# A hybrid decoder layer on one core: the sums of w_out's quarters, the norms' roots and the load of A12 placed anew

## The chip, the core and the metric

The kernel runs on one core of a Trainium2 chip, in float32. The metric is the device time of one execution in microseconds (us), the median of several executions. A program here issues instructions to TensorE (PE, matmuls; PEld is its weight load), VectorE (DVE), ScalarE (ACT), GpSimd (POOL) and SyncE (SP), which issues nearly all transfers (DMAs). Each engine works through its own queue in order.

## The reference, cut to what matters

```python
h = rms_norm(x, norm_gain) * (1.0 + scale) + shift          # shift, scale, gate from silu(c) @ W_ada + b_ada
proj = h @ w_in                                             # 1024x2048 @ 2048x8192
q_sb, k_sb, v_sb, z_sb, q_r, k_r, v_r, z_r = split(proj)    # 1024 columns each, 8 heads of 128
oa = stick_breaking_attention(rms_norm(q_sb), rms_norm(k_sb), v_sb) * silu(z_sb)
ob = head_group_norm(chunkwise_retention(rotary(q_r), rotary(k_r) * HD ** -0.5, v_r)) * silu(z_r)
y = concatenate([oa, ob]) @ w_out                           # 1024x2048 @ 2048x2048
return x + gate * y
```

## The kernel before, in words

**Products.** Every large product is float32 in three matmuls of 128x512 (`mm3`, L185 to L188): both factors are cut into a high and a low part (ScalarE copies the high part, VectorE subtracts it, L173 to L182), and high x high, high x low and low x high are added in PSUM. Both large products use a scheme of seven products of quarters in the place of eight: sums of quarters of the left and the right factor are multiplied. For the output, the right factor's quarters are B11, B12, B21 and B22 of w_out, and its sums T1 = B12 - B11, T2 = B22 - T1 = B22 - B12 + B11, T3 = B22 - B12 and T4 = B21 - T2. The left factor's quarters A11, A12, A21 and A22 are those of the concatenated heads, its sums S1 to S4.

**Order of the work.** TensorE's order is written out by hand. First come the norm and one seventh of the projection, then seven groups of columns (56 or more entries of 12 matmuls each, `run_entry`), then the output. Beside the groups' products run tasks that the clock of half steps (`tick`, twice an entry) pushes on: `later(n, fn)` enters `fn` n half steps later, ahead of the tasks of that half step and in the order in which it was asked for; a generator that yields n goes on n half steps later. The engines' queues hold instructions in the order in which they are entered so. The tasks are:

- `prepare(h)` (L970) and `sb_attention(h)` for the attention heads, two in each of groups 1 to 4. A score matmul of a head comes every three half steps; `scored` holds the half step of the last one, and whoever needs its PSUM bank A0 waits for `scored + 2`. `prepare` makes the norms of q and k: squares, sums over the partitions by matmul (`nm`), transposes (`ntp`), and in `roots` (L1011) an inverse square root by a first guess and three Newton steps of three small VectorE operations each (`rsqrt_newton`, L160). Four half steps after the transposes `y` is transposed itself (L1022).
- `sb_attention`: scores; one half step later sigmoids on ScalarE, three later `products` (L1112) on VectorE; `turn` (L1129) transposes the weights into banks B and A1, whose high and low parts are cut one and two half steps later (`lows`, L1161, with L1164).
- `gate_steps` (L883): the row of gates, from group 1 on. `bias_steps` (L851), from group 2 on: the bias of one column block in two halves, each with 16 loads, sums on VectorE (L864), one matmul per head (`zs`, L872) and copies (L874 to L878). At its end follow `sum_steps` (L938): for each of 8 row blocks k and 2 column blocks m, it loads B22, B12 and B11 of w_out (L946), makes T3, T1 and T2 (L950) and stores each to DRAM (L952).
- `ret_heads`: the eight retention heads, after the attention heads, from group 5 on (`ret_attention`, L1271, 21 half steps a head). Loads come six half steps before their rotation on VectorE (L1250 to L1255); `chain` (L1311, L1317) makes the states that `values` (L1336, L1343) multiplies; `stats` copies the result (L1348) and sums it, `roots` (L1360) and `norm` finish it, and a store to `concat` (L1383) frees its slot.
- `pump` (L262) loads the factors of the coming entries (L273, L275, and L260 through `load_raw`) whenever slots are free.

**Slots.** 92 slots of 128x512 are dealt in classes ("att" 30, "raw" 24, "ring" 24, "dst" 14) and given out first in, first out. A slot is put back when its last use is entered, so a new tile waits for the old one's last reader, a store too. An empty class "att" or "dst" borrows from the fullest.

**The output** has 64 steps (L1445): product 7 (T3) in two column halves of 8 steps, 12 matmuls a step; then products 1 (B11), 6 (T2), 5 (T1), 3 (B22), 2 (B21) and 4 (T4) of 8 steps, 24 matmuls a step. At step i the loads of the right factor for step i + 6 are issued (`load_right`, L1471), sums for step i + 4 made (`sum_right`, L1483; before only T4 = B21 - T2), and cuts for step i + 3 (`cut_right`, `cut_left`). `plan` (L1546) sets at which step the quarters A are loaded, multiplied with silu(z) (`times_z`) and summed (`left_sum`). Finished banks are copied or added (`evac_o`, L1643), with the last operations in `fin`.

Of the kernel before, what the change touches and what calls it, by code (L numbers as in the profile page):

```python
# [11 lines left out]
F32 = mybir.dt.float32  # L12
# [5 lines left out]
P = 128  # L18
S = 1024
# [32 lines left out]
class Slots:  # L52
# [25 lines left out]
    def get(self, name, cls=None, dtype=F32, borrow=False):  # L78
        q = self.free.get(cls) or self.free[None]
        if not q and (borrow or self.loose or cls in ("att", "dst")):  # L80
            q = max(self.free.values(), key=len)
        assert q, (name, cls, {c: len(f) for c, f in self.free.items()})
        i = q.popleft()
        t = self.pool.tile([P, HALF], dtype, tag=f"s{i}", name=name)
        self.of[id(t)] = (t, i)
        return t

    def put(self, *tiles):
        for t in tiles:
# [9 lines left out]
def layer_kernel(ctx, tc, x, c, w_ada, b_ada, norm_gain, w_in, sb_q_gain, sb_k_gain, ret_norm_gain, w_out,  # L99
# [18 lines left out]
    proj = {f"{n}{h}": dr.tile([P, S], F32, name=f"pr_{n}{h}") for n in ("q", "k", "z", "v", "rk", "rv")  # L118
            for h in range(NH)}
    krow = [dr.tile([1, S], F32, name=f"krow{h}") for h in range(NH)]  # L120
    sums_o = {(n, k): dr.tile([P, S], F32, name=f"sum_{n}_{k}") for n in ("T1", "T2", "T3") for k in range(8)}
    fac = {(n, k): dr.tile([P, 2, HALF], F32, name=f"fac_{n}_{k}") for n in RIGHT.values() for k in range(8)}

    def halves(hf):
        return slice(hf * HALF, (hf + 1) * HALF)
# [34 lines left out]
    def rsqrt_newton(y, m, u, iters=3):  # L160

        nc.vector.tensor_scalar(y.bitcast(I32), m.bitcast(I32), -0.5, RSQRT_MAGIC, op0=ALU.mult, op1=ALU.add)
        for _ in range(iters):
            nc.vector.tensor_tensor(u, y, y, op=ALU.mult)
            nc.vector.scalar_tensor_tensor(u, u, -0.5, m, op0=ALU.mult, op1=ALU.mult)
            nc.vector.scalar_tensor_tensor(y, u, 1.5, y, op0=ALU.add, op1=ALU.mult)

    w_in_k = w_in[0].rearrange("(k p) n -> p k n", p=P)

# [8 lines left out]
    def split_to(src, name, cls=None):  # L178

        hi, lo = get(f"{name}h", cls, F32R), get(f"{name}l", cls, F32R)  # L180
        nc.scalar.activation(hi, src, AF.Copy)
        nc.vector.tensor_tensor(lo, src, hi.bitcast(F32), op=ALU.subtract)  # L182
        return hi, lo
# [15 lines left out]
    def later(n, fn):  # L199
        due.setdefault(clock[0] + n, []).append(fn)  # L200
# [650 lines left out]
    def bias_steps():  # L851

        for i in range(2):
            n = min(HALF, NZ * P - i * HALF)
            acc = get(f"qb_acc{i}", "att", borrow=True)
            for kc in range(KC):
                raw = get(f"wb_{kc}_{i}", "att", borrow=True)
                nc.sync.dma_start(raw[:, 0:n], w_in[0][kc * P:(kc + 1) * P, rqcol + i * HALF:rqcol + i * HALF + n])
                yield 4
                a, r, by = acc[:, 0:n], raw[:, 0:n], shift[:, kc:kc + 1]  # L860
                if kc == 0:
                    nc.vector.tensor_scalar(a, r, by, None, op0=ALU.mult)
                else:
                    nc.vector.scalar_tensor_tensor(a, r, by, a, op0=ALU.mult, op1=ALU.add)  # L864
                put(raw)
                yield 1
            while clock[0] < scored[0] + 2:
                yield 1
            hs = slice(4 * i, min(NZ, 4 * i + 4))
            zs = ps.tile([P, NZ], F32, tag="A0", name=f"zs_{i}")  # L870
            for h in range(hs.start, hs.stop):
                nc.tensor.matmul(zs[:, h:h + 1], acc[:, h % 4 * P:(h % 4 + 1) * P], ones[:, 0:1],  # L872
                                 start=True, stop=True)
            nc.vector.tensor_copy(qb[:, 0, hs], zs[:, hs])  # L874
            put(acc)
            yield 2
            nc.scalar.activation(qb[0:64, 1, hs], qb[64:128, 0, hs], AF.Copy)
            nc.scalar.activation(qb[64:128, 1, hs], qb[0:64, 0, hs], AF.Copy)  # L878
        yield 2
        yield from sum_steps()  # L880
# [57 lines left out]
    def sum_steps():  # L938

        for k in range(8):  # L940
            for m in range(2):
                B = {}
                for n in ("B22", "B12", "B11"):
                    f, c_ = k + 8 * (n[1] == "2"), m + 2 * (n[2] == "2")
                    B[n] = get(f"s{n}_{k}_{m}", "att", borrow=True)
                    nc.sync.dma_start(B[n], w_out[0][f * P:(f + 1) * P, halves(c_)])  # L946
                yield 6
                for n, o, a, b, op in (("T3", "B22", "B22", "B12", ALU.subtract),
                                       ("T1", "B12", "B12", "B11", ALU.subtract), ("T2", "B11", "B22", "B11", ALU.add)):
                    nc.vector.tensor_tensor(B[o], B[a], B[b], op=op)  # L950
                    yield 2
                    nc.sync.dma_start(sums_o[n, k][:, halves(m)], B[o])  # L952
                    yield 2
                put(*B.values())

    def run_apart(gen):

# [12 lines left out]
    def prepare(h):  # L970
# [40 lines left out]
        def roots():  # L1011
            u = sm.tile([P, 16], F32, tag="u16", name=f"u16_{h}")
            nc.vector.tensor_scalar(m, m, EPS, None, op0=ALU.add)
            rsqrt_newton(y[:, 0:16], m, u)
            nc.vector.tensor_scalar(y[:, 16:24], y[:, 0:8], -1.0, None, op0=ALU.mult)

        later(1, roots)
        yield 4
        while clock[0] < scored[0] + 2:
            yield 1  # L1020
# [250 lines left out]
    def ret_attention(h, r, gap):  # L1271
# [87 lines left out]

        def roots():  # L1360
            m = sm.tile([P, 8], F32, tag="m8", name=f"m8_{h}")
            nc.vector.tensor_scalar(m, mv[:, :, 1], EPS, None, op0=ALU.add)
            y = sm.tile([P, 8], F32, tag="y8", name=f"y8_{h}")
            u = sm.tile([P, 8], F32, tag="u8", name=f"u8_{h}")
            rsqrt_newton(y, m, u)
            nc.vector.scalar_tensor_tensor(u, mv[:, :, 0], -1.0, y, op0=ALU.mult, op1=ALU.mult)

            def norm(g):
                for j in range(4):
                    i, sl = 4 * g + j, slice(j * P, (j + 1) * P)  # L1370
                    nc.scalar.activation(ons[g][:, sl], ons[g][:, sl], AF.Identity, scale=y[:, i:i + 1],
                                         bias=u[:, i:i + 1])
            later(3, lambda: norm(0))
            later(4, lambda: norm(1))

        def finish(g):
            on = ons[g]
# [82 lines left out]
    def load_s(n, k, m):  # L1460
        t = anywhere(f"w{n}_{k}_{m}")
        nc.sync.dma_start(t, sums_o[n, k][:, halves(m)])
        return t
# [7 lines left out]
    def load_right(i):  # L1471
        if i >= len(steps):
            return
        prod, ms, k = steps[i]
        for m in ms:
            if prod in (1, 2, 3):
                rraw[i, m] = [load_b({1: "B11", 2: "B21", 3: "B22"}[prod], k, m)]
            elif prod == 4:
                rraw[i, m] = [load_b("B21", k, m), load_s("T2", k, m)]
            else:  # L1480
                rraw[i, m] = [load_s({5: "T1", 6: "T2", 7: "T3"}[prod], k, m)]

    def sum_right(i, m):  # L1483

        if i < len(steps) and steps[i][0] == 4:
            a, b = rraw[i, m]
            nc.vector.tensor_tensor(a, a, b, op=ALU.subtract)
            put(b)

    def cut_right(i, m):  # L1490
        if i >= len(steps) or m not in steps[i][1]:
            return
        t = rraw.pop((i, m))[0]
        rcut[i, m] = split_to(t, f"r{i}_{m}", "any")
        put(t)

# [51 lines left out]
    def at(i, fn, *args):  # L1548
        plan.setdefault(i, []).append((fn, args))

    LOADS, SUMS, CUTS = 6, 4, 3
    for k in range(8):
        if k >= 6:
            at(k - LOADS, load_a, "A11", k)
            at(k - LOADS, load_a, "A21", k)
        if k >= 4:
            at(k - 4, left_sum, "S3", k)
        at(10 + k, load_a, "A11", k)
        at(12 + k, load_a, "A21", k)
        at(12 + k, load_a, "A22", k)  # L1560
        at(14 + k, load_a, "A12", k)
        at(15 + k, times_z, "A22", k)
        at(17 + k, left_sum, "S1", k)
        at(18 + k, times_z, "A12", k)
        at(20 + k, left_sum, "S2", k)
        at(27 + k, left_sum, "S4", k)
        at(56 + k - LOADS, load_a, "A22", k)
# [140 lines left out]
    for i, (prod, ms, k) in enumerate(steps):  # L1708
# [96 lines left out]
```

## Time and profile before

| | |
|---|---|
| median of 3 runs (lowest, highest) | 1939.34 us (1934.46, 1940.98) |
| the profiled execution's own time | 1942.26 us |
| its span | 1940.5 us |
| granted TensorE clock, mean | 0.992 |
| DMA | 541.00 MB, mean 279 GB/s |
| output stage, from 1655 to 1705 us | TensorE busy 50.00 of 50 us |

The page gives the busy time of each engine, what each waited for, and the chain of work that ended last. A row of waits reads: engine, line, tile, what it waited for, then total us, times, longest. A row in order of time reads: start, duration, engine, line, operation, result and operands, shape, count, and in brackets the idle time before it with what ended it. A row of windows reads: stretch, its length, busy time of each engine with instructions, granted clock, share of the DMA engines, GB/s. A duration of a matmul is its own, from start to end; matmuls overlap, so their spacing is what counts.

### The profile page before, as it was taken

Reading aid. Unit: us, or ns where it says so; the run is one execution under the profiler, and the core shown is the slowest. Engines: PE = TensorE matmul, PEld = TensorE weight load, DVE = VectorE, ACT = ScalarE, POOL = GpSimd, SP = SyncE. Lnnn points to the kernel's source line nnn. Section 1 sums busy time; section 2 is a strip of 40 time slices with the busy share of each in tenths; the row PEclk is TensorE's granted clock in tenths of the full one; section 3 lists DMA queues with packets and bytes.
Section 4 is the critical chain, followed back from the end, with each engine's and each line's share of the span. In section 5 each row is a group of like instructions: output and inputs, shape, how many; then the busy total and the mean of one; then the engine's idle time right before and its main releaser. Section 6 shows DMA issues by size and latency. Waiting matters only on the chain.

```text
span 1940.5 us, 28542 instructions
## 1 busy us (share of the span) xinstructions
PE 1876.2 (97%) x9511; PEld 1541.4 (79%) x9511; DVE 1334.2 (69%) x2587; ACT 833.7 (43%) x1568; POOL 86.2 (4%) x278
## 2 busy tenths in 40 slices
PE   5999999999999999999999999998899999999998
PEld 3777778878788877887888788886778888888887
DVE  4637765446768786877788777976667756564769
ACT  5437852234544454444544454333323455443231
POOL 0000000000010010001000111000000000000000
PEclk9999999999999999999999999998999999999999
DMA  9969997997798789977998989998997883943594
GB/s 317 357 210 314 324 334 252 282 352 245 249 297 290 263 271 296 310 278 252 313 351 293 319 292 336 328 316 273 336 352 222 275 264 121 372 147 103 171 311 163
DMA packets 411823, 541.00 MB, mean 279 GB/s; under 512 B 34078, under 2 KB 207512, under 8 KB 411676
## 3 DMA queue, kind: packets, MB, share of 16 engines
q1 hardware_dynamic: 411144, 539.01, 83.4%
q8 instruction: 75, 1.23, 0.3%
q14 instruction: 72, 0.59, 0.1%
q10 hardware_dynamic: 532, 0.17, 0.0%
HBM read 448.83 MB, written 90.22 MB: 278 GB/s over the span
## 4 chain that ended last, share of the span: by engine, by line
PE 43%; DVE 4%; DMA 4%; issue 0%; ACT 0%; SPq 0%; DVEq 0%; ACTq 0%
PE pj L186 8%; PE pj L187 8%; PE pj L188 8%; PE y L186 4%; PE y L187 4%; PE y L188 4%; DMA sw_q<-rqraw 1%; DMA sw_k<-pr_rk 1%; PE op L1343 1%; PE op L1341 1%; DVE wl L175 1%; PE sp L1325 1%; DMA xr<-in_x_dram 1%; PE up L1307 0%; PE oT L188 0%
## 5 line engine op out<-in xcount | busy, mean ns | idle before, releaser
L175 DVE TENSOR_TENSOR wl<-A,wh 128x512 fp32r<-128x512 f32 x392 | 272.7, 696 | 255.1 <-ACT wh L173 235.4
L173 ACT ACTIVATE wh<-A 128x512 fp32r<-128x512 f32 x392 | 246.6, 629 | 358.4 <-PE pj L187 338.9
L389 ACT ACTIVATE c<-pj 128x512 f32<-128x512 f32 x112 | 66.6, 598 | 185.7 <-PE pj L188 151.3
L392 DVE TENSOR_TENSOR c<-pj,c 128x512 f32<-128x512 f32 x112 | 75.0, 687 | 56.8 <-PE pj L188 56.2
L296 DVE TENSOR_TENSOR A<-A,A 128x512 f32<-128x512 f32 x160 | 109.6, 694 | 1.7
L1119 DVE TENSOR_TENSOR_SCAN om<-om 128x128 f32<-128x128 f32 (+2 forms) x96 | 93.7, 976 | 1.1
L186 PE MATMUL first<-h_hi,wh_first 128*128 128x512 f32 x224 | 92.4, 412 | 1.1 <-ACT h_hi L596 1.1
L186 PE MATMUL pj<-B21h,wh 128*128 128x512 f32 x232 | 93.0, 401 | 0.1
L186 PE MATMUL pj<-T1h,wh 128*128 128x512 f32 x232 | 92.8, 400 | 0.0
L186 PE MATMUL pj<-B11h,wh 128*128 128x512 f32 x232 | 92.4, 398 | 0.0
L186 PE MATMUL pj<-B22h,wh 128*128 128x512 f32 x232 | 92.2, 398 | 0.0
L188 PE MATMUL pj<-B21h,wl 128*128 128x512 f32 x232 | 91.4, 394 | 0.0
L187 PE MATMUL pj<-B21l,wh 128*128 128x512 f32 x232 | 91.0, 392 | 0.0
L187 PE MATMUL pj<-B11l,wh 128*128 128x512 f32 x232 | 91.0, 392 | 0.0
L188 PE MATMUL pj<-B11h,wl 128*128 128x512 f32 x232 | 90.9, 392 | 0.0
L188 PE MATMUL pj<-T1h,wl 128*128 128x512 f32 x232 | 90.8, 391 | 0.0
L187 PE MATMUL pj<-T1l,wh 128*128 128x512 f32 x232 | 90.7, 391 | 0.0
L188 PE MATMUL pj<-B22h,wl 128*128 128x512 f32 x232 | 90.6, 391 | 0.0
L187 PE MATMUL pj<-B22l,wh 128*128 128x512 f32 x232 | 90.5, 390 | 0.0
L188 PE MATMUL pj<-T3h,wl 128*128 128x512 f32 x224 | 88.1, 393 | 1.8 <-DVE wl L175 1.8
L186 PE MATMUL pj<-T4h,wh 128*128 128x512 f32 x224 | 89.6, 400 | 0.0
L186 PE MATMUL pj<-T3h,wh 128*128 128x512 f32 x224 | 88.7, 396 | 0.9 <-ACT wh L173 0.9
(388 smaller groups left out, 4938.3 us busy)
## 6 DMA issues: line engine op xcount, KB each, us to landing
A<-in_w_in_dram SPq DMA_DIRECT2D x228, 256.0 KB, 5.5
ada<-in_w_ada_dram SPq DMA_DIRECT2D x128, 256.0 KB, 5.8
gr<-in_w_ada_dram SPq DMA_DIRECT2D x64, 256.0 KB, 5.3
wT<-sum_T SPq DMA_DIRECT2D x64, 256.0 KB, 5.3
wB<-in_w_out_dram SPq DMA_DIRECT2D x64, 256.0 KB, 4.7
T2h<-fac_T SPq DMA_DIRECT2D x56, 256.0 KB, 5.6
T2l<-fac_T SPq DMA_DIRECT2D x56, 256.0 KB, 5.0
T1h<-fac_T SPq DMA_DIRECT2D x56, 256.0 KB, 5.5
```

Source lines behind the costliest of these rows:

```text
L173: nc.scalar.activation(hi[:, 0:n], src[:, 0:n], AF.Copy)
L175: nc.vector.tensor_tensor(lo[:, 0:n], src[:, 0:n], hi[:, 0:n].bitcast(F32), op=ALU.subtract)
L186: nc.tensor.matmul(o, a_hi, b_hi, start=first, stop=False, skip_group_check=on)
L187: nc.tensor.matmul(o, a_hi, b_lo, start=False, stop=False, skip_group_check=on)
L188: nc.tensor.matmul(o, a_lo, b_hi, start=False, stop=last, skip_group_check=on)
L296: nc.vector.tensor_tensor(r[o], r[a], r[b], op=ALU.add if n == 1 else ALU.subtract)
L389: nc.scalar.activation(t, o, AF.Copy)
L392: nc.vector.tensor_tensor(dst[q, cc], o, dst[q, cc], op=ALU.add)
L1119: nc.vector.tensor_tensor_scan(rev, rev, rev, init, op0=ALU.mult, op1=ALU.bypass)
L1325: nc.tensor.matmul(sp[:, j, :], r["k", g][:, tk], r["q", g][:, tk], start=True, stop=True)
L1341: nc.tensor.matmul(op[:, j, :], pT[:, tk], vb(i), start=True, stop=(i == 0))
L1343: nc.tensor.matmul(op[:, j, :], qd[:, tk], state(i), start=False, stop=True)
```

## The change

- `sum_steps` makes and stores T3 alone, from two loads. T1 and T2 are made in the output: T1 from loads of B12 and B11, T2 from a load of T3 and one of B11. T2 is stored when it is cut, for T4 later. `sum_right` makes all sums that have two loads.
- The three Newton steps of `prepare` and of a retention head come in three half steps in the place of one; the retention head's `norm` comes one half step later.
- In `bias_steps`, three half steps pass before the bank is asked for, and the copy out of it is entered one half step after the matmuls.
- In the output A12 is loaded seven steps later and multiplied six steps later. In a step that does the work of two, each step's sums are now made for that step's own column blocks.

```diff
-    sums_o = {(n, k): dr.tile([P, S], F32, name=f"sum_{n}_{k}") for n in ("T1", "T2", "T3") for k in range(8)}
+    sums_o = {(n, k): dr.tile([P, S], F32, name=f"sum_{n}_{k}") for n in ("T2", "T3") for k in range(8)}
...
+    def rsqrt_guess(y, m):
         nc.vector.tensor_scalar(y.bitcast(I32), m.bitcast(I32), -0.5, RSQRT_MAGIC, op0=ALU.mult, op1=ALU.add)
+    def newton(y, m, u):
+        nc.vector.tensor_tensor(u, y, y, op=ALU.mult)
+        nc.vector.scalar_tensor_tensor(u, u, -0.5, m, op0=ALU.mult, op1=ALU.mult)
+        nc.vector.scalar_tensor_tensor(y, u, 1.5, y, op0=ALU.add, op1=ALU.mult)
...
+            yield 3
             while clock[0] < scored[0] + 2:
                 yield 1
...
+            put(acc)
+            yield 1
             nc.vector.tensor_copy(qb[:, 0, hs], zs[:, hs])
-            put(acc)
             yield 2
...
-                B = {}
-                for n in ("B22", "B12", "B11"):
-                    f, c_ = k + 8 * (n[1] == "2"), m + 2 * (n[2] == "2")
-                    B[n] = get(f"s{n}_{k}_{m}", "att", borrow=True)
-                    nc.sync.dma_start(B[n], w_out[0][f * P:(f + 1) * P, halves(c_)])
+                a, b = [get(f"s{j}_{k}_{m}", "att", borrow=True) for j in range(2)]
+                for t, f in ((a, k + 8), (b, k)):
+                    nc.sync.dma_start(t, w_out[0][f * P:(f + 1) * P, halves(m + 2)])
                 yield 6
-                for n, o, a, b, op in (("T3", "B22", "B22", "B12", ALU.subtract),
-                                       ("T1", "B12", "B12", "B11", ALU.subtract), ("T2", "B11", "B22", "B11", ALU.add)):
-                    nc.vector.tensor_tensor(B[o], B[a], B[b], op=op)
-                    yield 2
-                    nc.sync.dma_start(sums_o[n, k][:, halves(m)], B[o])
-                    yield 2
-                put(*B.values())
+                nc.vector.tensor_tensor(a, a, b, op=ALU.subtract)
+                put(b)
+                yield 2
+                nc.sync.dma_start(sums_o["T3", k][:, halves(m)], a)
+                put(a)
+                yield 2
...
-        later(1, roots)
+        u = sm.tile([P, 16], F32, tag="u16", name=f"u16_{h}")
+        def roots(i):
+            if i == 0:
+                nc.vector.tensor_scalar(m, m, EPS, None, op0=ALU.add)
+                rsqrt_guess(y[:, 0:16], m)
+            newton(y[:, 0:16], m, u)
+            if i == 2:
+                nc.vector.tensor_scalar(y[:, 16:24], y[:, 0:8], -1.0, None, op0=ALU.mult)
+        for i in range(3):
+            later(1 + i, lambda i=i: roots(i))
         yield 4
...
-            rsqrt_newton(y, m, u)
-            nc.vector.scalar_tensor_tensor(u, mv[:, :, 0], -1.0, y, op0=ALU.mult, op1=ALU.mult)
+            rsqrt_guess(y, m)
+            newton(y, m, u)
+            later(1, lambda: newton(y, m, u))
+            def last():
+                newton(y, m, u)
+                nc.vector.scalar_tensor_tensor(u, mv[:, :, 0], -1.0, y, op0=ALU.mult, op1=ALU.mult)
+            later(2, last)
...
-            later(3, lambda: norm(0))
-            later(4, lambda: norm(1))
+            later(4, lambda: norm(0))
+            later(5, lambda: norm(1))
...
-            elif prod == 4:
+            elif prod == 7:
+                rraw[i, m] = [load_s("T3", k, m)]
+            elif prod == 6:
+                rraw[i, m] = [load_s("T3", k, m), load_b("B11", k, m)]
+            elif prod == 5:
+                rraw[i, m] = [load_b("B12", k, m), load_b("B11", k, m)]
+            else:
                 rraw[i, m] = [load_b("B21", k, m), load_s("T2", k, m)]
-            else:
-                rraw[i, m] = [load_s({5: "T1", 6: "T2", 7: "T3"}[prod], k, m)]
...
-        if i < len(steps) and steps[i][0] == 4:
+        if i < len(steps) and len(rraw[i, m]) == 2:
             a, b = rraw[i, m]
-            nc.vector.tensor_tensor(a, a, b, op=ALU.subtract)
+            nc.vector.tensor_tensor(a, a, b, op=ALU.add if steps[i][0] == 6 else ALU.subtract)
...
         t = rraw.pop((i, m))[0]
+        if steps[i][0] == 6:
+            nc.sync.dma_start(sums_o["T2", steps[i][2]][:, halves(m)], t)
...
-        at(14 + k, load_a, "A12", k)
+        at(21 + k, load_a, "A12", k)
...
-        at(18 + k, times_z, "A12", k)
+        at(24 + k, times_z, "A12", k)
...
-            for m in ms:
-                sum_right(i + d + SUMS, m)
+            if i + d + SUMS < len(steps):
+                for m in steps[i + d + SUMS][1]:
+                    sum_right(i + d + SUMS, m)
```

More of the change, by code (lines that the diff above doesn't have):

```diff
@@ L158, in layer_kernel, with rsqrt_newton @@
     ret_g = cols[:, 50:58]
-    def rsqrt_newton(y, m, u, iters=3):
+    def rsqrt_guess(y, m):
         nc.vector.tensor_scalar(y.bitcast(I32), m.bitcast(I32), -0.5, RSQRT_MAGIC, op0=ALU.mult, op1=ALU.add)
[L163 to L166, printed above, removed]
+    def newton(y, m, u):
+        nc.vector.tensor_tensor(u, y, y, op=ALU.mult)
+        nc.vector.scalar_tensor_tensor(u, u, -0.5, m, op0=ALU.mult, op1=ALU.mult)
+        nc.vector.scalar_tensor_tensor(y, u, 1.5, y, op0=ALU.add, op1=ALU.mult)
+    def rsqrt_newton(y, m, u):
+        rsqrt_guess(y, m)
+        for _ in range(3):
+            newton(y, m, u)
     w_in_k = w_in[0].rearrange("(k p) n -> p k n", p=P)
@@ L1009, in prepare @@
                              AF.Copy, scale=1.0 / HD)
[L1011 to L1015, printed above, removed]
-        later(1, roots)
+        u = sm.tile([P, 16], F32, tag="u16", name=f"u16_{h}")
[8 more added lines that the diff above has]
+            later(1 + i, lambda i=i: roots(i))
         yield 4
@@ L1361, in roots @@
             m = sm.tile([P, 8], F32, tag="m8", name=f"m8_{h}")
-            nc.vector.tensor_scalar(m, mv[:, :, 1], EPS, None, op0=ALU.add)
             y = sm.tile([P, 8], F32, tag="y8", name=f"y8_{h}")
             u = sm.tile([P, 8], F32, tag="u8", name=f"u8_{h}")
-            rsqrt_newton(y, m, u)
-            nc.vector.scalar_tensor_tensor(u, mv[:, :, 0], -1.0, y, op0=ALU.mult, op1=ALU.mult)
+            nc.vector.tensor_scalar(m, mv[:, :, 1], EPS, None, op0=ALU.add)
+            rsqrt_guess(y, m)
+            newton(y, m, u)
+            later(1, lambda: newton(y, m, u))
+            def last():
+                newton(y, m, u)
+                nc.vector.scalar_tensor_tensor(u, mv[:, :, 0], -1.0, y, op0=ALU.mult, op1=ALU.mult)
+            later(2, last)
             def norm(g):
```

## The prediction

> **What bounds the kernel now.** I read the head of the page first, then what TensorE waited for, then its order of time at the longest waits.
>
> ```profile
> span 1940.5 us, 28542 instructions
> PE 1876.2 (97%) x9511; PEld 1541.4 (79%) x9511; DVE 1334.2 (69%) x2587; ACT 833.7 (43%) x1568; POOL 86.2 (4%) x278
> ```
>
> TensorE is busy 97% of the span, and the change removes no matmul. So only TensorE's idle time, and time in which its clock is reduced, can be won. The waits after the start, in us (total, times, longest):
>
> ```profile
> PE op L1343 <- DVE state L1317: 18.2, 3, 9.5
> PE tp_B L1139 <- DVE om L1116: 6.8, 4, 2.2
> PE zs L872 <- ACT wh L173: 2.0, 1, 2.0
> PE nm L993 <- DVE qb L874: 0.5, 1, 0.5
> PE zp L186 <- ACT ga L920: 0.6, 2, 0.4
> ```
>
> The first row is the case. Its three waits in the order of time, and then, from the chain of work, at which spacing matmuls ran after them (start, us):
>
> ```profile
> 1332.42 0.79 PE L1343 MATMUL op<-state,rq 128*128 128x128 f32 x2 [9.46 <-DVE state L1317]
> 1382.19 0.80 PE L1343 MATMUL op<-state,rq 128*128 128x128 f32 x2 [4.91 <-DVE state L1317]
> 1456.52 0.80 PE L1343 MATMUL op<-state,rq 128*128 128x128 f32 x2 [3.84 <-DVE state L1317]
> ```
>
> ```profile
> 1336.13 0.23 PE pj L186
> 1386.83 0.42 PE pj L188
> 1387.25 0.23 PE pj L186
> 1462.39 0.23 PE pj L188
> ```
>
> A 512 column matmul normally takes 0.23 us. After each wait it takes 0.43, until 1336.13, 1387.25 and 1462.39: 3.7, 5.1 and 5.9 us at half rate, of which half, 7.3 us, is lost. Idle 18.2 plus 7.3 makes **25.5 us** that hang on these three waits, all in the retention heads of one stage. Why there? By stage (us, busy times, granted clock, DMA share, GB/s):
>
> ```profile
> 918.00:1218.00 300.00, 296.41 (x1504) 245.21 (x1503) 231.16 (x422) 141.00 (x273) 25.05 (x103) 1.00 0.94 315
> 1218.00:1450.00 232.00, 217.00 (x1105) 183.36 (x1104) 166.47 (x348) 76.10 (x137) 11.16 (x8) 0.96 0.98 320
> 1475.00:1630.00 155.00, 155.00 (x843) 132.96 (x842) 98.63 (x240) 71.46 (x129) 10.02 (x7) 1.00 0.75 236
> 1655.00:1705.00 50.00, 50.00 (x222) 41.40 (x222) 33.59 (x56) 18.58 (x34) 0.00 (x0) 1.00 1.03 378
> 1705.00:1850.00 145.00, 145.00 (x642) 120.09 (x641) 87.62 (x141) 49.09 (x89) 0.00 (x0) 1.00 0.41 134
> ```
>
> From 1218 to 1450 the DMA engines are full (0.98); from 1475 to 1630 four retention heads run at 0.75, and TensorE is busy throughout. What stood behind the waits (ScalarE, SyncE's queue and VectorE in order of time):
>
> ```profile
> 1321.65 0.46 SPq L1383 DMA_DIRECT2D concat<-on  x1
> 1327.26 0.60 ACT L1348 ACTIVATE on<-op 128x512 f32<-128x512 f32 x1 [15.42 <-DMA concat<-on]
> 1372.14 0.60 ACT L389 ACTIVATE c<-pj 128x512 f32<-128x512 f32 x1 [10.48 <-DMA pr_rk<-c]
> 1442.02 0.69 DVE L1253 TENSOR_TENSOR sw_k<-sw_k,sin 128x512 f32<-128x512 f32 x1 [6.72 <-DMA sw_k<-pr_rk]
> ```
>
> Each time an engine that works in order stood before one late transfer: two copies waited for a store that was to free their slot, one rotation for its load. Everything behind them on ScalarE and VectorE, the next cuts and the states among it, came late, and then TensorE. The first store was issued only at 1321.65: the queue itself lags.
>
> **The change, part by part.** First the sums in the groups.
>
> ```profile
> L950 DVE TENSOR_TENSOR sB<-sB,sB x48: 678/685/779, 920.7 to 1429.0; 128x512 f32<-128x512 f32 x48
> L946 SPq DMA_DIRECT2D sB<-in_w_out_dram x48: 327/340/834, 903.3 to 1412.1; - x48
> ...
> DMA packets 55217, 74.15 MB, mean 320 GB/s; under 512 B 4849, under 2 KB 25169, under 8 KB 55200
> sum_T<-sB SPq DMA_DIRECT2D x21, 256.0 KB, 5.4
> sB<-in_w_out_dram SPq DMA_DIRECT2D x18, 256.0 KB, 6.0
> ```
>
> (The last three rows are of 1218 to 1450.) Sixteen pairs of three loads, three additions and three stores go in steps of 6 + 3 x 4 = 18 half steps. From the first load, 903.3, to the last store, about 1442, a pair takes 33.7 us, a half step 1.87. The new pair has 10 half steps, 18.7 us, two loads, one addition, one store. The start moves 8 half steps (15 us) back, as the two halves of the bias each get four more; so the sums end near 918 + 16 x 18.7 = 1217. Until then they send 3 transfers in 18.7 us instead of 6 in 33.7, which is nearly the same; after it none. From 1218 to 1450 that takes out 21 + 18 = 39 transfers of 0.262 MB, 10.2 of the 74.15 MB. Without stalls the stage would last 232 - 25.5 = 206.5 us. Before, it would need 74.15 MB / 206.5 us = 359 GB/s, and it got 320. After, 63.9 / 206.5 = 310 GB/s, which is what 918 to 1218 carries (315) with no wait of this kind. Also one slot less is held while a pair runs, and none after 1217, so that a copy gets a slot whose store is older.
>
> Worth: from nothing to 25.5. I take it that the first two waits go whole: 9.46 + 4.91 + (3.7 + 5.1) / 2 = 18.8. For the third I count half of its idle time, 1.9, and its half rate, 2.9: its loads come in a burst at the beginning of the last group, which stays. Together **-23.6**. VectorE gets 32 x 0.685 = 21.9 us less in the groups, which alone is worth nothing, as TensorE waits there for transfers.
>
> On the clock, the Trainium skill ("TensorE: Matmul & The Clock Gate", Part 1) says that the array falls to half rate after an idle window of about 3.4 us and returns after a busy one. By that rule the three waits lose 3 x 3.4 / 2 = 5.1 us, an estimate, and the sum would be 2.2 smaller; the rows above, up to 5.9 us slow, decide here.
>
> **The norms' roots**, 12 small operations in one half step, are put over three.
>
> ```profile
> 506.20 0.17 DVE L1013 TENSOR_SCALAR m<-m 128x16 f32<-128x16 f32 x1
> 508.49 0.17 DVE L1015 TENSOR_SCALAR y<-y 128x8 f32<-128x8 f32 x1
> 511.29 0.61 DVE L1164 TENSOR_TENSOR al<-tp_B,ah 128x256 fp32r<-128x256 f32 x2
> 512.05 0.41 PE L1139 MATMUL tp_B<-ident,be 128*128 128x128 f32 x2 [1.54 <-DVE om L1116]
> ```
>
> They take 2.37 us, and the transposes that wait at 512.05 need the bank that L1164 reads at 511.29. The roots are entered at the half step T+3 after a score, and the lows of L1164 at T+5. The new parts come at T+3, T+4 and T+5, and the third is entered one half step before the lows, so it runs ahead of them. VectorE has no gap between 503.5 and 511.9, so the same 2.37 us still lie before L1164. I count **0** of the 6.8 us; bounds: -6.8 if they fall behind the lows, +0.8 if the first head's transpose of y, one half step behind the last part, has to wait. Only before the longest of the four, at 1114, an addition of the sums (0.6) stood in that chain too: -0.6. The eight roots of a retention head are spread in the same way, where no wait of TensorE hangs on them: 0.
>
> **The bias sum** gets three more half steps before its matmul:
>
> ```profile
> 755.52 0.78 DVE L864 SCALAR_TENSOR_TENSOR qb_acc<-wb,shift,qb_acc 128x512 f32<-128x512 f32 x1
> ```
>
> The matmul zs waited 2.0 us for this operation, the last of its sum; three half steps are 5.6 us, in which other products go on. **-2.0**. The copy of zs out of its bank is entered one half step later, in the one in which the next score may use the bank; the gate's copy has that pattern and cost 0.6 in two. I add +0.6 for two, and +0.8 for y above.
>
> **The output** gets what the groups lose: 16 more loads each for T1 and T2, 16 stores of T2, 32 additions. The output is 1344 matmuls, 222 in 50 us, so, ending at 1935, it begins near 1632; steps 18 to 35, which carry the new work, lie from 1687 to 1784. At steps 21 to 28 up to 8 transfers fall on a step of 24 matmuls (5.4 us): 2.1 MB, 388 GB/s, against 378 seen at 1655 to 1705, where A12's loads, now seven steps later, were part of the crowd; from 1705 on the share was 0.41. The lag is then 0.15 us a step, some 1 us. A load has two steps, 10.8 us, before its addition, and the cut is used three steps later. VectorE:
>
> ```profile
> 1695.00:1712.00 17.00, 15.57 (x27) 1.00 0.82 296
> 1678.49 0.94 SPq L1462 DMA_DIRECT2D wT<-sum_T  x2
> 1701.81 0.69 DVE L182 TENSOR_TENSOR r_0l<-wT,r_0h 128x512 fp32r<-128x512 f32 x1
> SPq L1462 <- PE y L188: 24.4, 7, 9.1
> ```
>
> It is nearly full before (15.6 of 17), because the products of A12 and A22 fall together; the first go six steps later, and two additions come: 9 operations a step at 0.6, 5.4 of 5.4 us. The first cut of T2 at 1701.8 is three steps before its use. A lag of two steps is covered; the queue's waits for slots (24.4) eat part of the load's lead only. So **0**; bounds 0 and, were all 32 additions on the path, +19.2.
>
> **Sum:** -23.6 - 0.6 - 2.0 + 0.6 + 0.8 = -24.8. The profiled execution took 1942.26 us, the span and 1.8 around it, 2.9 above the median of the runs shown, 1939.34. Against the median: 1939.3 - 24.8 = **1915 us**.
>
> **The rivals.** (1) The roots do release the transposes, by an order that I read wrongly: 6.8 less, 1908. For it: they are the largest block in that chain; against it: no gap on VectorE.
>
> (2) The stage stays short of transfers. 310 GB/s against 320 reached is little room, and retention's loads have six half steps only. Half of the 25.5 stays: 1915 + 12 = 1927. The Trainium skill ("DMA: Bandwidth & Descriptors", Specifications) gives a core some 358 GB/s of HBM. By that figure the stage's 74.15 MB fit 207 us already, the waits would be of order and not of amount, and less traffic alone would mend only part: an estimate that leans to this rival. The rows do not decide it: 378 was carried at 1655, 320 here at a share of 0.98.
>
> (3) The wait moves: what the stage wins is given back where the sums are now made, the third wait growing or the cuts of T2 coming late: 1936 to 1942.
>
> (4) Slower: the circle of 1321 forms in the output. If a load of B11 or B12 lands later than two steps after its issue, VectorE stands before its addition, the stores of T2 behind it hold SyncE's queue, and the next loads come later still. One such circle cost 9.46 + 1.85 = 11.3 us; three give 34: 1949. It decides from a lag of 10.8 us; for it speak the 24.4 us of waits for slots in this queue, against it the share of 0.41.
>
> **How the numbers follow.** Forecast 0.57, (1) 0.08, (2) 0.18, (3) 0.08, (4) 0.09. A measurement of this kernel tells 0.3%, 5.8 us, from no change: faster is below 1933.5. That holds for the forecast, (1) and nearly all of (2): 0.80; within it most of (3) and the end of (2): 0.11; slower (4): 0.09. The range goes from below (1) to behind (2), 1906 to 1936, about 0.82.
>
> **What would show it.** Right: no sums after about 1220; a share near 0.94 in the retention stage; op L1343 waits under 4 us in all and no clock below 1.00 there; tp_B L1139 still waiting some 6 us at four places; zs without a wait; TensorE without a gap in the output, VectorE near full from 1695 to 1760. Wrong: waits of y on r_0l or r_1l, waits of VectorE for wB or wT, retention stalls that merely moved.

## The result and the profile after

The changed kernel took 1920.07 us, median of 4 runs (1919.4 to 1921.47), the kernel before 1939.51 us, also of 4 (1934.46 to 1940.98). The ratio is 0.9905, 95% interval 0.9886 to 0.9924: **0.95% faster**, 19.4 us. The profiled execution took 1920.55 us, against 1942.26 before. The prediction said 1915 us with a range of 1906 to 1936.

Line numbers shift: the state's product is L1343 before and L1354 after, the transposes L1139 and L1150, the subtraction behind them L1164 and L1175, the copy of zs L874 and L884. The head of the page after:

```profile
span 1918.5 us, 28552 instructions
PE 1869.8 (97%) x9511; PEld 1535.3 (80%) x9511; DVE 1329.6 (69%) x2587; ACT 835.0 (44%) x1568; POOL 81.7 (4%) x278
```

VectorE is busy nearly as long as before (1329.6 against 1334.2 us): the additions were moved, not removed. What TensorE waited for in the kernel after (total us, times, longest):

```profile
PE tp_B L1150 <- DVE om L1127: 5.4, 4, 1.9
PE tp_B L1150 <- DVE al L1175: 2.9, 4, 2.2
PE nm L999 <- ACT be L1115: 2.8, 1, 2.8
PE zp L193 <- ACT be L1115: 2.0, 2, 1.7
...
PE zp L193 <- DVE qb L884: 1.5, 1, 1.5
...
PE yp L1033 <- DVE y L167: 1.0, 2, 0.6
...
PE op L1354 <- DVE state L1328: 0.5, 1, 0.5
```

The state's row fell from 18.2 us to 0.5, and the wait of zs is gone. The four waits at the bank behind `om` still stand (6.8 before, 5.4 now). Two rows are new and were in no term of the sum, nm and zp behind ScalarE's `be`. Two more are new and were counted, zp behind the copy of zs (`qb`) and yp behind `y`. The windows of the kernel after, in four of the same stretches:

```profile
918.00:1218.00 300.00, 291.69 (x1478) 240.74 (x1477) 219.06 (x403) 137.68 (x267) 23.71 (x101) 1.00 0.92 305
1218.00:1450.00 232.00, 231.36 (x1205) 195.60 (x1204) 176.45 (x387) 85.88 (x156) 11.94 (x9) 1.00 0.94 300
1655.00:1705.00 50.00, 50.00 (x222) 41.40 (x221) 41.85 (x70) 20.93 (x38) 0.00 (x0) 1.00 1.02 358
1705.00:1850.00 145.00, 145.00 (x642) 120.05 (x641) 103.54 (x168) 45.13 (x81) 0.00 (x0) 1.00 0.67 221
```

The second row is the gain: TensorE 231.36 of 232 us where it was 217, the clock 1.00 where it was 0.96, 1205 matmuls in place of 1105. The first row shows what was paid: TensorE busy 291.69 us against 296.41. The last two take up the sums: VectorE 41.85 in place of 33.59 us in 50, the DMA engines at 0.67 in place of 0.41, and TensorE without a gap. It has no wait from 1640 us on.

Where the time came from is read best from the starts of one product in both kernels. Three of them, first of the kernel before, then of the kernel after: B21 of group 3, T4 of group 4, and the first matmul of the output.

```profile
757.33 0.48 PE L186 MATMUL pj<-B21h,wh 128*128 128x512 f32 x1
...
1216.57 0.39 PE L186 MATMUL pj<-T4h,wh 128*128 128x512 f32 x1
...
1629.30 0.48 PE L186 MATMUL y<-r_0h,l0h 128*128 128x512 f32 x1
```

```profile
751.86 0.39 PE L193 MATMUL pj<-B21h,wh 128*128 128x512 f32 x1
...
1220.47 0.39 PE L193 MATMUL pj<-T4h,wh 128*128 128x512 f32 x1
...
1607.28 0.48 PE L193 MATMUL y<-r_0h,l0h 128*128 128x512 f32 x1
```

The kernel after is 5.5 us ahead at the first, 3.9 **behind** at the second, 22.0 ahead at the third, and stays so to the end. So three stretches: -5.5, then +9.4 lost, then -25.9 won between 1217 us and the output. The loss hardly shows in the totals of the page; it shows where starts are compared. About 0.9 us of it is no loss: zs's first matmuls stand ahead of the first mark before (756.45) and behind it after (756.84).

### The profile page after: what moved, and what is told of

It reads as the page before. It is cut to its first block, busy times and chain, and to the rows that moved or that the text cites. A ratio compares the mean times of both kernels' runs of the same rounds, so it can differ in the third digit from the quotient of the medians.

```text
span 1918.5 us, 28552 instructions
## 1 busy us (share of the span) xinstructions
PE 1869.8 (97%) x9511; PEld 1535.3 (80%) x9511; DVE 1329.6 (69%) x2587; ACT 835.0 (44%) x1568; POOL 81.7 (4%) x278
## 4 chain that ended last, share of the span: by engine, by line
PE 41%; DMA 5%; DVE 4%; issue 1%; ACT 0%; SPq 0%; DVEq 0%; ACTq 0%
PE pj L193 8%; PE pj L195 8%; PE pj L194 8%; PE y L194 4%; PE y L193 4%; PE y L195 4%; DMA wB<-in_w_out_dram 1%; DMA xr<-in_x_dram 1%; PE sp L1336 1%; PE op L1352 1%; PE op L1354 1%; PE up L1318 1%; DVE wl L182 1%; DMA B21h<-fac_B 0%; PE ktp L1310 0%
## 5 line engine op out<-in xcount | busy, mean ns | idle before, releaser
L193 PE MATMUL pj<-T2h,wh 128*128 128x512 f32 x224 | 89.5, 399 | 0.2 <-DMA T2h<-fac_T 0.2
```

Of the source, the lines that this page charges most:

```text
L193: nc.tensor.matmul(o, a_hi, b_hi, start=first, stop=False, skip_group_check=on)
```

## The experiments

Each comparison is with the kernel before on the same chip: 1937.36 us (31 runs) for `sums_only`, `roots_only`, `traffic` and `slots`, 1935.88 (8) for `again`, `put_late`, `all_three` and `a12_early`, 1936.76 (19) for the other four. None leaves a part of the computation out; `traffic` and `slots` add work or hold tiles that nothing uses. For each, the starts of the same three products are given against the kernel before's profile, as a triple; for the kernel after it is (-5.5, +3.9, -22.0). A triple is of one execution, and so is what it is compared with: the kernel before's profiled execution was 2.8 us above its median.

### Which part carries the gain

**`sums_only`**: the change with the roots and the bias undone.

```diff
-            yield 3
             while clock[0] < scored[0] + 2:
...
-            put(acc)
-            yield 1
             nc.vector.tensor_copy(qb[:, 0, hs], zs[:, hs])
+            put(acc)
...
-        for i in range(3):
-            later(1 + i, lambda i=i: roots(i))
+        later(1, roots)
```

> The new sums and the new place of A12 alone; roots and bias as before. If the sums carry the gain by what they take out of the retention stage: 1918 to 1924 us, states waited for under 3 us in all, the bank of the bias sum waited for 2.0 us again. If the roots or the bias carry part of it: 1926 or more.

1930.24 us, ratio 0.9966 [0.9956, 0.9977]. By time alone the sums carry a third of the gain. By the triple (-1.3, +13.5, -11.7) they carry all that is gained between 1217 and the output, -25.2 us, and the kernel loses 14.8 between 757 and 1217. What TensorE waited for there, and ScalarE in order of time just before the longest, with SyncE's queue:

```profile
1104.54 0.32 SPq L956 DMA_DIRECT2D sum_T<-s  x1
```

```profile
1110.23 0.60 ACT L1001 ACTIVATE nr<-nm 128x512 f32<-128x512 f32 x1 [6.68 <-DMA sum_T<-s]
```

```profile
1110.88 0.50 PE L193 MATMUL zp<-k_0h,q_1h 128*128 128x512 f32 x1 [3.70 <-ACT nr L1001]
```

Here the cause has its own name. ScalarE's copy `nr` goes into a slot that a store of T3, issued at 1104.54, still reads. The changed `sum_steps` puts that slot back in the line behind the store's issue; the kernel before waited two half steps after its last store before it put its three slots back. ScalarE stands for 6.68 us, and TensorE for 3.70.

**`roots_only`**: the kernel before with the three parts in `prepare` alone.

```diff
-        later(1, roots)
+        for i in range(3):
+            later(1 + i, lambda i=i: roots(i))
```

> The kernel before, with the roots of the attention heads alone put over three half steps. If the third part runs ahead of the lows that free the bank, as the order says: 1936 to 1942 us, the transposes into bank B still waiting 6 to 7 us for VectorE. If the roots release them: 1932 to 1935 us and waits of 2 us.

1937.28 us, ratio 1.0001 [0.9986, 1.0015]. The transposes still wait:

```profile
PE tp_B L1151 <- DVE om L1128: 6.2, 4, 1.9
```

Roots by themselves are worth nothing. Its triple is (-3.4, +1.0, -1.8): it too is 4.3 later over the middle stretch, so that part of the change's +9.4 may be the one execution of the kernel before.

### Traffic or slots

The prediction gave two reasons for the gain in the retention stage: fewer transfers, and fewer slots held. Each was given back alone.

**`traffic`**: 42 copies of quarters of w_out from DRAM to DRAM after the sums, 0.262 MB each, with no slot.

```diff
+        for i in range(42):
+            f, c_ = i % 16, i // 16
+            scr = dr.tile([P, HALF], F32, name=f"scr_{i}")
+            nc.sync.dma_start(scr, w_out[0][f * P:(f + 1) * P, halves(c_)])
+            yield 3
```

> The changed kernel, and after its sums 42 transfers of 256 KB from DRAM to DRAM, one every three half steps, which hold no slot and which nobody waits for. They bring the number of transfers between about 1218 and 1450 us back to that of before. If the amount of transfers makes the retention waits: 1930 to 1945 us, states waited for 8 us or more. If held slots make them: 1919 to 1923 us, no such wait.

**`slots`**: three slots held over the same half steps, with no transfer.

```diff
+        held = [get(f"held{i}", "att", borrow=True) for i in range(3)]
+        yield 126
+        put(*held)
```

> The changed kernel, and after its sums three slots of the attention class are held for 126 half steps without any transfer, from about 1215 to 1450 us. If the amount of transfers makes the retention waits: 1919 to 1923 us, as changed. If scarce slots make them (a copy gets a slot whose store is young): 1926 or more, with copies waiting for stores to concat.

`traffic` took 1935.45 us, ratio 0.9987 [0.9972, 1.0002]; `slots` 1931.68, 0.9977 [0.9964, 0.999]. The state's row of the waits and the retention stage's window, of `traffic` first, then of `slots`:

```profile
PE op L1359 <- DVE state L1333: 8.1, 2, 4.1
```

```profile
1218.00:1450.00 232.00, 221.89 (x1133) 186.83 (x1133) 164.04 (x352) 80.19 (x145) 10.80 (x8) 0.98 1.02 335
```

```profile
PE op L1357 <- DVE state L1331: 9.6, 2, 6.8
```

```profile
1218.00:1450.00 232.00, 222.29 (x1143) 188.63 (x1143) 167.00 (x359) 79.81 (x144) 10.89 (x9) 0.98 0.92 292
```

With full DMA engines (1.02) and no slot held, 8.1 us of waits come back; with engines that have room (0.92, 292 GB/s) and three slots fewer, 9.6. Their triples are (-6.8, +2.9, -7.8) and (-5.2, +7.0, -6.9): over the stretch to the output `traffic` gives back 15.3 of the 25.9 us, `slots` 12.0. `traffic` puts back a little more than was taken out, 335 GB/s where the kernel before had 320, so its share is on the high side. So both reasons are real, and neither alone makes the whole. But they are not apart. In front of the two waits of `traffic` stand a store that was to free a slot (ScalarE) and a load (VectorE):

```profile
1363.98 0.60 ACT L396 ACTIVATE c<-pj 128x512 f32<-128x512 f32 x1 [11.19 <-DMA pr_rk<-c]
...
1434.63 0.69 DVE L1269 TENSOR_TENSOR sw_k<-sw_k,sin 128x512 f32<-128x512 f32 x1 [8.48 <-DMA sw_k<-pr_rk]
```

In `slots` both are stores that free a slot:

```profile
1331.17 0.60 ACT L1362 ACTIVATE on<-op 128x512 f32<-128x512 f32 x1 [12.71 <-DMA concat<-on]
...
1374.86 0.60 ACT L396 ACTIVATE c<-pj 128x512 f32<-128x512 f32 x1 [8.29 <-DMA pr_rk<-c]
```

The second fence shows the two waits of the kernel before (15.42 and 10.48) come back with nothing else changed than three idle tiles. The first shows that transfers alone bring back one of them, and the late load too: stores that land later also keep their slots longer.

**`early_sums`**: the kernel before with its pairs in 10 half steps, so that all three sums end before the retention stage.

```diff
-                yield 6
+                yield 4
...
-                    yield 2
+                    yield 1
                     nc.sync.dma_start(sums_o[n, k][:, halves(m)], B[o])
-                    yield 2
+                    yield 1
```

> The kernel before, with all three sums, but a pair in 10 half steps in the place of 18, so that they end near 1215 us. If only the stage in which they run counts: states waited for under 5 us from 1218 to 1450, and 1920 to 1930 us. If the amount counts wherever it is: the DMA engines are full from 918 to 1218, new waits of 10 us or more stand there, 1934 us or more.

1941.36 us, ratio 1.0023 [1.0012, 1.0033]: slower. The retention stage is nearly as good as with the change, the attention stage much worse:

```profile
PE tp_B L1139 <- DVE al L1164: 11.9, 5, 4.5
...
PE op L1343 <- DVE state L1317: 1.5, 1, 1.5
```

```profile
918.00:1218.00 300.00, 280.35 (x1383) 230.15 (x1384) 225.79 (x410) 129.62 (x252) 23.87 (x96) 0.98 0.96 324
1218.00:1450.00 232.00, 230.15 (x1194) 194.82 (x1192) 173.42 (x364) 86.15 (x156) 12.87 (x16) 1.00 0.98 309
```

The triple (+1.4, +27.2, +2.4) has -24.9 in the one stage and +25.8 in the one ahead of it. Within the groups the sums can only be pushed about; that the change moves two of three into the output, where the DMA engines stood at 0.41, is what pays.

### What was lost in the middle

**`again`** is the changed kernel once more, for a comparison on the same chip.

> The changed kernel itself, beside the next three: 1919 to 1922 us.

1923.62 us (1915.23 to 1924.71, 4 runs), ratio 0.9925 [0.9898, 0.9953], a median above the 1919 to 1922 that were expected. Its profiled execution is the fastest of the four, with the triple (-8.4, -1.7, -27.3): 6.7 us lost in the middle, where the first execution lost 9.4. A difference of some 3 us in one stretch between two single traces proves nothing here.

**`put_late`**: T3's slot is put back two half steps after its store.

```diff
                 nc.sync.dma_start(sums_o["T3", k][:, halves(m)], a)
-                put(a)
                 yield 2
+                put(a)
```

> The changed kernel, with the slot of T3 put back two half steps after its store is issued, as the kernel before did, in the place of at once. If the waits of ScalarE in the groups with the sums (4.1 us at 1100) are for that store: 1912 to 1917 us, and neither nm nor the score at 1100 to 1110 waits over 0.5 us. If they are only a matter of full DMA engines: 1918 to 1922 us, the same waits.

1916.2 us (1914.44 to 1919.95), ratio 0.9899 [0.9878, 0.9921]. In the kernel after, SyncE's queue, ScalarE and TensorE around 1100 us:

```profile
1094.22 0.46 SPq L958 DMA_DIRECT2D sum_T<-s  x1
```

```profile
1100.49 0.55 ACT L1166 ACTIVATE ah<-tp_A 128x256 fp32r<-128x256 f32 x2 [4.13 <-DMA B22h<-fac_B]
```

```profile
1101.83 0.64 PE L999 MATMUL nm<-qs,ones 128*32 128x256 f32 x8 [2.79 <-ACT be L1115]
```

In `put_late`, ScalarE at the same operations:

```profile
1091.89 0.60 ACT L1166 ACTIVATE ah<-tp_B 128x512 fp32r<-128x512 f32 x1 [1.31 <-PE tp_B L1150]
1092.38 0.55 ACT L1166 ACTIVATE ah<-tp_A 128x256 fp32r<-128x256 f32 x2
```

The wait of 4.13 us is gone, and TensorE's of 2.79 (2.35 in `again`) with it. The profile had named the load B22h as the releaser; that only the time of T3's `put` was changed shows that it was T3's store, issued 6.3 us before the end of the wait. The order of `get` and `put` in kernel.py says the same: this `ah` is the next tile in the slot that T3's tenth store, that of 1094.22, hands on, and in `put_late` it gets another slot. In the time it is less clear: 7.4 us below `again` by the medians, but the intervals overlap, and the two traces differ by 0.9 us over the middle stretch (+5.8 against +6.7). It has the lowest median of all, and is the version that I would keep, though the runs don't show it to be faster than the change.

**`all_three`**: `put_late`, the copy of zs back behind its matmuls, and the roots entered three half steps later, behind the lows that the transposes wait for.

```diff
-            yield 1
             nc.vector.tensor_copy(qb[:, 0, hs], zs[:, hs])
...
-            later(1 + i, lambda i=i: roots(i))
-        yield 4
+            later(4 + i, lambda i=i: roots(i))
+        yield 8
```

> put_late, the three parts of the attention heads' roots four, five and six half steps after the transposes in the place of one, two and three (so behind the lows that free the bank), and the copy of zs entered in the half step of its matmuls again. If the bank waits for whatever stands ahead of the lows: the four waits of the transposes into bank B fall from 5.4 us together to under 1.5, 1906 to 1912 us. If VectorE is simply full there and the work only moves: those waits stay over 4 us or others of 3 us and more appear, 1913 to 1920 us.

1920.18 us, ratio 0.9925 [0.99, 0.995]: no better. The four waits behind `om` are gone, as roots behind the lows had to show. But the transposes into the same bank now wait 8.2 us in four for the lows themselves (`al`, 2.9 in the kernel after), nm 5.2 in three for `be`, and others stand elsewhere, as the second of these:

```profile
987.46 0.66 PE L1149 MATMUL tp_B<-ident,be 128*128 128x128 f32 x2 [3.58 <-DVE al L1174]
...
1443.38 0.49 PE L1353 MATMUL op<-state,rq 128*128 128x128 f32 x2 [3.57 <-DVE state L1327]
```

Its triple (-4.3, +1.7, -13.0) is short of `put_late`'s (-8.0, -2.3, -27.9) in the retention stage above all. Its profiled execution was its slowest (1929.22), so that the size of this is not to be trusted; that waits moved is shown.

**`put_copy`**: `put_late` and the copy of zs back, without the roots' move.

```diff
-            yield 1
             nc.vector.tensor_copy(qb[:, 0, hs], zs[:, hs])
```

> put_late, and the copy of zs entered in the half step of its matmuls again, so that the next score no longer meets it. 1912 to 1917 us if the wait of 1.5 us of the score near 910 goes and nothing takes its place; 1916 to 1920 us if it only moves.

1917.9 us, ratio 0.9902 [0.9888, 0.9917], triple (-4.6, +1.8, -23.5). The score's wait at 912 is gone, and a transpose of 2.08 us at 936 stands in its place. The copy's extra half step is no cost to be won back alone.

### The bias, the roots and A12

**`no_bias`**: the change with the bias part undone.

```diff
-            yield 3
             while clock[0] < scored[0] + 2:
...
-            put(acc)
-            yield 1
             nc.vector.tensor_copy(qb[:, 0, hs], zs[:, hs])
+            put(acc)
```

> The changed kernel with the bias sum as before: no three half steps ahead of its matmuls, and sums that begin eight half steps earlier. If the bias makes the difference between the sums alone and the whole change: 1925 to 1932 us, zs waiting 2 us or more with matmuls at half rate behind it, and a tile that waits for the store of T3 at another place than 1100. If the roots make it: 1918 to 1923 us.

1931.9 us, ratio 0.9977 [0.9966, 0.9988], the triple (-4.9, +9.3, -15.0). The waits of TensorE that stand for it:

```profile
PE zp L193 <- ACT nr L1001: 4.2, 1, 4.2
...
PE zs L879 <- ACT wh L180: 2.2, 1, 2.2
```

By the ratios the bias part is worth 0.5% (beside `again`) to 0.7%, some 10 to 14 us, not 2. Its own wait is 2.2; but its three and one half steps, twice, are also what starts the sums eight half steps later (the first store of T3 at 937.2, here at 917.3), and with the earlier start a store of T3 meets `nr`, as in `sums_only`. Another store meets a cut here, ScalarE's in order of time:

```profile
934.50 0.60 ACT L1164 ACTIVATE ah<-tp_B 128x512 fp32r<-128x512 f32 x1 [6.96 <-DMA gate_row<-ga]
```

TensorE's next transposes into the bank waited 3.55 us behind it (938.68), and 3.20 in `sums_only`, where ScalarE waited 6.60 for the same store. This slot, of the row of gates, is put back at its store's issue in every one of these kernels; which tile gets it hangs on the order of the tasks. 14.2 us are lost from 757 to 1217 here, 9.4 and 6.7 in the two traces of the changed kernel.

**`no_roots`**: the change with one block of roots, in `prepare` and in the retention heads.

```diff
-        for i in range(3):
-            later(1 + i, lambda i=i: roots(i))
+        later(1, roots)
```

> The changed kernel with all roots in one half step again. If the split of the roots is worth nothing: 1917 to 1924 us, the transposes into bank B waiting 6 to 7 us, the transposes of y not at all. If it makes the difference of 10 us between the sums alone and the whole change: 1927 or more.

1918.67 us, ratio 0.991 [0.9887, 0.9933], triple (-9.9, -1.7, -26.4). Beside the changed kernel's two results that is the same: also within the change the roots bring nothing.

**`a12_early`**: A12 loaded and multiplied as before.

```diff
-        at(21 + k, load_a, "A12", k)
+        at(14 + k, load_a, "A12", k)
...
-        at(24 + k, times_z, "A12", k)
+        at(18 + k, times_z, "A12", k)
```

> The changed kernel with A12 loaded and multiplied at its old steps, so that its loads, the two quarters more and the products fall together in the output. If VectorE and the queue have two steps of slack there: 1919 to 1923 us, no wait of TensorE from 1640 on. If the seven steps were needed: 1924 or more, waits of y on the cuts from 1700 to 1760.

1920.78 us, ratio 0.9925 [0.99, 0.9949], and no wait of TensorE from 1640 on. The seven steps weren't needed either: the output hides A12's loads in both orders.

## Why the prediction was right, point by point

- **The retention stage, -23.6**: -25.9, and 24.4 to 25.6 in seven other runs with the new sums and nothing put back (in `all_three`, slow in its profile, 14.7). The two reasons held, each for about half when it was given back alone. The third wait went whole, of which I had left 1.9; two executions differ by more than that here (the stretch of `roots_only`, with 17.2 us of the state's waits, is 2.8 shorter than that of the kernel before). The stage carried 300 GB/s at 0.94, where 310 was worked out; the last store of T3 was issued at 1210.0, where the sums were to end near 1217.
- **Rival (2)**, half of the stalls stay, is what either reason alone would have left: `traffic` and `slots` both stand there. The page that leaned to it (the Trainium skill, "DMA: Bandwidth & Descriptors", Specifications, some 358 GB/s a core) gives the right order of the limit: the fullest windows carried 335 GB/s (`traffic`), 358 (the output after) and 378 (before), the last above it. But the waits are of amount too, where that estimate leaned to order alone: `traffic` brings them back. And `slots` waits at 292 GB/s, so a rate alone doesn't tell whether a stage stalls.
- **Roots, 0**: right in value (`roots_only`, `no_roots`) and by its reason. The third part still ends just ahead of the lows; VectorE and then TensorE in the kernel after:

```profile
507.53 0.17 DVE L1025 TENSOR_SCALAR y<-y 128x8 f32<-128x8 f32 x1
507.61 0.61 DVE L1175 TENSOR_TENSOR al<-tp_B,ah 128x256 fp32r<-128x256 f32 x2
```

```profile
508.37 0.41 PE L1150 MATMUL tp_B<-ident,be 128*128 128x128 f32 x2 [1.29 <-DVE om L1127]
```

  Rival (1) would have needed them behind the lows. `all_three` put them there, and its waits came up elsewhere, so that even then 1908 would not have come.
- **The zs wait, -2.0**: gone, as worked out.
- **The output, 0**: right. From its first matmul to the end of the span the output takes 311.2 us in both kernels. VectorE took the additions with TensorE never waiting, so rivals (3) and (4) did not come.
- **What groups 3 and 4 lose, +0.6 and +0.8**: this step failed. It was 9.4 in the profile (6.7 in `again`), and it is the main reason why the time is 1920 and not 1915. TensorE's waits in this stretch come to 11.3 us after and 5.7 before, 5.6 more; half rate adds 1.4 (below), zs's own matmuls 0.9 by the mark alone, and some 1.5 stand in none of these. y's transposes waited 1.0 us in two, near the 0.8, but the first (0.57 at 637) lies ahead of this stretch. The copy of zs did not cost the gate's 0.6: one wait of 1.46, and half rate behind it. The wait of zp for `be`, 1.72 at 959, stands behind a copy of ScalarE that waited for the store of an earlier tile of its slot:

```profile
957.47 0.60 ACT L396 ACTIVATE c<-pj 128x512 f32<-128x512 f32 x1 [5.91 <-DMA pr_q<-c]
```

  And the largest single wait, 2.79 at 1101, is of an edit that the prediction read past: that T3's slot is put back at its store's issue. The prediction counted one slot less held, and took that for a gain alone. The bias part, costed at its own wait, moves the start of the sums and with it which tiles meet a store.
- **Not foreseen, -3.4**: the first 450 us ran faster after, from 442 us on by 3.4, with nothing of the change before them but the roots. `no_roots`, without these, is 6.1 ahead there (436.53), and `early_sums` 1.4 behind at 757, so this differs between executions and is put down to no edit. That it makes up for a part of the loss above is luck.

The terms as measured from start to start: -3.1 up to 723 us, -2.4 from there to 757 with zs's wait in it, +9.4, -25.9. They make -22.0 at the output's start. The two profiled executions differ by 21.7 and the medians by 19.4.

**What stays open**: why eight half steps earlier cost so much more in the middle. That a store of T3 then meets `nr` is shown for one wait of about 4 us in `sums_only` and in `no_bias`, and that the gates' store meets `ah` for one of 3.55 and 3.20; the rest of the 14 us is not shown. The bias part was not put alone into the kernel before. `traffic` and `slots` together were not tried, so how the two add is not shown; apart they give back 15.3 and 12.0, together 27.3 of 25.9.

## What to carry to other kernels

When a stage stalls with its DMA engines full, move work into a stage with idle DMA time: moved into the stage next door, which is nearly as full, it costs there what it gains here. Count the slots beside the bytes, and the half step at which a slot is put back: one handed on as its store is issued makes the next writer, and all that its engine has queued, wait for that store. And an edit that only adds half steps also shifts all that follows it on the same task; compare the starts of the same products in both traces, stage by stage, since a total hides a loss of 9 us under a gain of 26.

## What the runs showed of the hardware

Half rate came after less idle time than I had expected, and not each time. In the kernel after, TensorE at the copy of zs:

```profile
910.16 0.41 PE L1150 MATMUL tp_B<-ident,be 128*128 128x128 f32 x2 [0.60 <-DVE om L1127]
910.40 0.38 PE L1150 MATMUL tp_A<-ident,be 128*128 128x128 f32 x2
912.25 0.44 PE L193 MATMUL zp<-k_1h,q_1h 128*128 128x384 f32 x1 [1.46 <-DVE qb L884]
...
913.43 0.63 PE L195 MATMUL pj<-T1h,wl 128*128 128x512 f32 x1
913.86 0.63 PE L193 MATMUL pj<-T1h,wh 128*128 128x512 f32 x1
...
916.42 0.49 PE L193 MATMUL pj<-T1h,wh 128*128 128x512 f32 x1
```

The spacing is 0.43 us from 913.43 to 916.42, seven matmuls, where 0.23 is normal: 1.4 us lost behind two waits of 0.60 and 1.46 with four transposes between them. The granted clock was 0.50 from 913.4 to 916.4. The same place in `again`, which is the same kernel:

```profile
906.71 0.41 PE L1150 MATMUL tp_B<-ident,be 128*128 128x128 f32 x2 [0.59 <-DVE om L1127]
908.80 0.45 PE L193 MATMUL zp<-k_1h,q_1h 128*128 128x384 f32 x1 [1.46 <-DVE qb L884]
...
910.14 0.39 PE L193 MATMUL pj<-T1h,wh 128*128 128x512 f32 x1
910.37 0.40 PE L194 MATMUL pj<-T1l,wh 128*128 128x512 f32 x1
```

The waits are the same, the spacing stays at 0.23 us and the granted clock at 1.00 (910 to 913). So neither the length of these waits nor their sum decides. The Trainium skill ("TensorE: Matmul & The Clock Gate", Part 1) speaks of an idle window of about 3.4 us; in the kernel after 2.06 us of idle time within 2.7 came ahead of half rate, and the measurement decides. The same section calls that window free-running; by that, where in it the waits fall could make the difference. The two executions fit this, but no run here shows the window itself.
